# Chunk outputs added into y by accumulating transfers, and the gate row spread through DRAM, in a one-core SSD and gating-MLP layer

## The chip, the core and the metric

The kernel runs on one core of a Trainium2 chip. The metric is the time of one execution on the device in microseconds (us). The engines are PE (TensorE, matmuls into PSUM), DVE (VectorE), ACT (ScalarE), POOL (GpSimd) and SP (SyncE, which here only issues transfers). POOL and ACT issue transfers too.

## The reference, cut to what matters

One layer mixes 256 latent tokens (width 2048) with a prefix of 256 context tokens. An input projection feeds two groups of heads: a bidirectional Mamba-2 SSD (32 heads of 64, 8 groups of 4 heads) and a gating MLP. Both go through one output projection.

```python
zx = hx @ w_in                                   # f32; every product here is f32
xbc = silu(dwconv5(z[..., :XBC_W]))              # x heads, B, C of the SSD
# SSD in chunks of 128, per head, forward and backward:
y_diag = einsum('bcgqk,bcgrqk,bckgrp->bcqgrp', CB, Lmat, xdt)
y_off  = einsum('bcqgn,bcgrpn,bcqgr->bcqgrp', Cc, h_starts, exp(acs))
y = y_diag + y_off                               # both directions summed
y = y + d_skip * xh
y_a = rmsnorm(y * silu(z_ssd), g_ssd)
...
shift, scale, gate = split(silu(c) @ w_ada + b_ada, 3)
out = x + gate * rmsnorm(concat([y_a, y_b]) @ w_out, g_post)
```

`Lmat` is the causal decay between the tokens of a chunk. The kernel takes `gate * g_post` as one row `G` of 2048 numbers, repeated over the 128 partitions.

## The kernel before

**Matmuls.** An f32 product is made of three fp32r matmuls: the weights and the activations are each split into a high part (ACT casts, L543 or L87) and a low part (DVE subtracts, L549 or L88), and hi x hi, hi x lo and lo x hi are summed. The whole program is a long row of such matmuls, and everything else is set beside it. Weights come in blocks of 1 MB on SP's queue, four in flight; halves of a block are split ahead of PE, with four buffers.

**Stages.** First the modulation and the first seven projection tiles (to about 121 us). Then the 25 remaining tiles of x, B and C (`REST`), 512 columns each (256 for the C tiles), one after another into two PSUM banks (`acp`, bufs=2). Then 16 blocks of the latent-only projections (v, u and the two gate paths), then the output projection.

**The SSD beside the projection.** Group g owns the tiles 4g to 4g+3: two of x, one of B, one of C. For each tile `conv_tile` sets a first tap (ACT, L608), the other taps (DVE, L624) and a SiLU (ACT, L627). Tiles 12, 13 and 15 were projected in the first stage and wait in SBUF (`zq`, which lies in y's memory). Each is then turned so that tokens are on partitions. Groups 0 and (mostly) 7 do that on PE; groups 1 to 6 by DVE's 32x32 transpose, a store to DRAM (`turn`, SP) and four loads back (`turned`, SP). Then, per group: `ssd_cb` and `ssd_states` on PE, `ssd_mb` on POOL (M, L897), `ssd_hd` on POOL (hs, L885), `ssd_hl` on DVE (L891), `ssd_m` on DVE (L905, L907), `ssd_o` on PE, `ssd_yo` on DVE, `ssd_ya` on POOL (adds into y, L935), `ssd_yd` on PE (the diagonal part, into `psy`). The diagonal part comes out with heads on partitions, so it is turned as well: `ssd_yc`, `ssd_yt`, and `ssd_yf` adds it to y (DVE, L972).

The decay of group g+1 is prepared in between. `row_load` (POOL, L725) spreads 1 MB of cumulative sums into the one buffer `R`; `ssd_d` (ACT, L821) subtracts; `ssd_min` (DVE, L828) takes the minimum of two directions; then `row_load` of the next group may go; `ssd_e` (ACT, L834) is the exponential.

**Order.** PE, DVE, ACT and POOL run in the order in which this stage issues. It is made by a clock of the kernel's own: `later(t, f)` puts f into a list, due at the present clock plus t, and after every six matmuls `pump` advances the clock by 1.3 (0.65 in the 256-column tiles) and issues what is due, earliest due first. `plan_tile` sets all due times of a tile and `plan_d`, `plan_e` those of the decay. An engine waits at an instruction until its inputs are there, and all that is behind it on that engine waits too. SP's order and, after this stage, that of the other engines but for PE's sequence in the code are chosen by the framework.

**The gate.** `gate_tile` makes 16 columns of gate values on DVE. `gate_bcast` (L1076 on) transposes them on PE, splits them into two parts on ACT and DVE, and in four steps (`spread`) multiplies a matrix of ones with them on PE, so that every partition gets the row; the result is multiplied into `G`, which held `g_post`.

**y** is a tile of 128 x 4 x 2 x 512 (four pairs of groups, two chunks, 512). Transfers in `lat_t` turn it later, blocks of 128 at a time.

Of the kernel before, what the change touches and what calls it, by code (L numbers as in the profile page):

```python
# [36 lines left out]
C_BADA, C_GPRE, C_GSSD, C_GMLP, C_BS, C_CW, C_CB, NPC = 0, 48, 64, 80, 96, 112, 272, 304  # L37
# [10 lines left out]
def tile_hybrid_ssd_mlp(  # L48
# [47 lines left out]
    y = ypool.tile([P, 4, 2, 512], F32, tag="big16", name="y")  # L96
# [35 lines left out]
    gate = cpool.tile([P, 48], F32, name="gate")  # L132
# [21 lines left out]
    def yseg(j):  # L154
        return y[:, j % 4, j // 4]
# [589 lines left out]
    def turned(dst, D):  # L745
        for b in range(4):
            nc.sync.dma_start(dst[32 * b : 32 * b + 32].rearrange("p (u c) -> p u c", c=32),
                                D[16 * b : 16 * b + 16, :].rearrange("u (i c) -> i u c", c=32))
# [75 lines left out]
    def ssd_min(g, c):  # L824
        R = rows_[g]
        if c == 0:
            gs_.setdefault(g, {})["E"] = cv1.tile([P, 2, 4, P], F32, tag="E", name=f"E{g}")
        nc.vector.tensor_tensor(gs_[g]["E"][:, c], R[:, :, 0, c, :], R[:, :, 1, c, :], op=ALU.min)  # L828
        if c == 1:
            row_load(g + 1)  # L830
# [78 lines left out]
    def yg(g, c):  # L909
        return y[:, g // 2, c, (g % 2) * 256 : (g % 2 + 1) * 256]  # L910
# [40 lines left out]
    def ssd_yc(g):  # L951
        S = gs_[g]
        S["yc"] = cv1.tile([P, 2, 2, P], F32, tag="M", name=f"yc{g}")
        if by_pe(g, "y"):
            nc.scalar.copy(S["yc"], S["psy"])
        else:
            S["Dy"] = turn(S["yc"].rearrange("p c q k -> p (c q k)"), S["psy"].rearrange("p c q k -> p (c q k)"), f"y{g}")

    def ssd_yt(g):
        S = gs_[g]  # L960
        if not by_pe(g, "y"):
            S["pty"] = cv1.tile([P, 2, 2, P], F32, tag="yo0", name=f"yz{g}")
            turned(S["pty"].rearrange("p c q k -> p (c q k)"), S["Dy"])
            return
        S["pty"] = spt([P, 2, 2, P], f"pty{g}")
        for c in range(2):
            for q in range(2):
                nc.tensor.transpose(S["pty"][:, c, q, :], S["yc"][:, c, q, :], ident)
# [7 lines left out]
    def plan_tile(i, src, d0=0.0, ds=5.2, tx=7.0, tw=1.5, late=0.0, td=0.0):  # L976
# [3 lines left out]
        lx, lb, ly = (0.7 if by_pe(g, w) else LAND for w in (f"x{r}", "b", "y"))  # L980
# [41 lines left out]
    plan_tile(12, zq[0], 70, ds=7, tx=9)  # L1022
# [52 lines left out]
    def gate_bcast():  # L1075
        gs.close()  # L1076
        gp = ctx.enter_context(mkpool(name="gp", bufs=1, side="right"))
        G = gp.tile([P, D], F32, name="G")
# [3 lines left out]
        nc.vector.tensor_copy(gate[:, 32:48], gate[:, 0:16])


        gh = gp.tile([48, P], F32R, name="gh")
        gl = gp.tile([48, P], F32R, name="gl")
        g1 = gp.tile([48, P], F32R, name="g1")
        gd = gp.tile([48, 4, P], F32R, name="gd")
        gk = gp.tile([48, KT], F32, name="gk")
        nc.scalar.copy(g1, ones[0:48])  # L1090
        nc.vector.tensor_tensor(gk, ident[0:48, 0:16], ident[0:48, 32:48], op=ALU.add)

        def rows():
            ps = spt([48, P], "psgt")
            nc.tensor.matmul(ps, lhsT=gate, rhs=ident, start=True, stop=True)
            nc.scalar.copy(gh, ps)
            nc.vector.tensor_tensor(gl, ps, gh.bitcast(F32), op=ALU.subtract)
            nc.vector.tensor_copy(gh[32:48], gl[32:48].bitcast(F32))

        def expand(j):  # L1100
            nc.vector.tensor_tensor(gd, bc(gh.bitcast(F32), 1, 4), bc(gk[:, 4 * j : 4 * j + 4], 2, P), op=ALU.mult)

        def spread(j):
            p = spt([P, 512], f"pg{j}")
            nc.tensor.matmul(p, lhsT=g1, rhs=gd, start=True, stop=True)
            gb = G[:, j * 512 : (j + 1) * 512]
            nc.vector.tensor_tensor(gb, p, gb, op=ALU.mult)
            if j < 3:
                expand(j + 1)

        later(2, rows)
        later(4, lambda: expand(0))
        for j in range(4):
            later(7 + 3 * j, lambda j=j: spread(j))

    def lat_t(kind, j4):
        src = (L_["vt"] if kind == 2 else y)[:, j4]
        T = L_["lt2"].tile([P, 1024], F32, tag="gw", name=f"T{kind}{j4}").rearrange("p (u c) -> p u c", c=P)
        for tk in range(2):
            nc.vector.transpose(T[:, 4 * tk : 4 * tk + 4].rearrange("p u c -> p (u c)"), src[:, tk])  # L1120
        dst = src.rearrange("p t (j c) -> p (t j) c", c=P)
        for a in range(4):
            for b in range(4):
                nc.gpsimd.dma_start(dst[32 * b : 32 * b + 32, :, 32 * a : 32 * a + 32],  # L1124
                                    T[32 * a : 32 * a + 32, :, 32 * b : 32 * b + 32])
# [245 lines left out]
_INS = ["xch", "xtok", "ccols", "crow", "wada", "pcols", "dtp", "dskip", "gpost", "gv", "wst", "wxbc", "wlat", "wsp", "wout"]  # L1371
# [72 lines left out]
```

## Time and profile before

| | us |
|---|---|
| median of 3 runs (968.04 to 968.32) | 968.29 |
| the profiled execution | 968.23 |
| its span | 966.5 |
| DMA issues of `yz<-Dy` (SP), median to landing | 2.6 |
| `ssd_yf`'s adds (DVE), median | 0.68 |

The span is the profile's; what lies between it and the execution's time (1.7 us) is start and end. Lines of the timeline give the start, the duration, the engine, the line of the kernel, the operation, the tiles (out<-in), the shape and the count; in brackets stand the idle time of that engine before it and what ended that. A matmul's duration is longer than the step to the next one, since matmuls overlap: to price matmuls, read from start to start.

### The profile page before, as it was taken

The page shows a single profiled execution, that of the slowest core. Times are in us where ns is not written, and L with a number is a line of the kernel's source. Part 1 is how long each engine was busy: PE and PEld are TensorE (multiplying, and loading weights), DVE is VectorE, ACT ScalarE, POOL GpSimd, SP SyncE. Part 2 cuts the span into 40 slices and gives each one's busy share as a digit, 9 for nine tenths or more (in the row PEclk, how much of TensorE's full clock was granted, in tenths as well). Part 3 has the DMA queues.
Part 4 walks back from the last instruction along what each step waited for, and adds up shares of the span by engine and source line. Part 5 has one row for each costly group of instructions (what it writes and reads, how often), then busy time and mean ns, then how long its engine had stood idle before and what let it go on. Part 6 is the DMA issues. An engine that isn't in the chain of part 4 may idle for free.

```text
span 966.5 us, 13778 instructions
## 1 busy us (share of the span) xinstructions
PE 954.9 (99%) x5142; PEld 771.1 (80%) x5142; DVE 686.7 (71%) x1116; ACT 482.2 (50%) x732; POOL 192.5 (20%) x290
## 2 busy tenths in 40 slices
PE   9999999999999999999999999999999999999997
PEld 4688888777787878787888888887888888888885
DVE  6888798879887877866667687767666665445636
ACT  4344458554555544455445333455566564346512
POOL 0000002532533414323000000043335440000000
PEclk9999999999999999999999999999999999999999
DMA  9999965566659767647877767785666666556722
GB/s 367 416 416 415 371 228 166 145 187 156 136 151 229 170 179 163 164 143 248 317 295 281 285 259 273 285 302 197 198 226 214 215 214 216 198 181 255 261 87 87
DMA packets 141490, 224.57 MB, mean 232 GB/s; under 512 B 110816, under 2 KB 111072, under 8 KB 118768
## 3 DMA queue, kind: packets, MB, share of 16 engines
q1 hardware_dynamic: 134640, 206.03, 63.2%
q0 software_dynamic: 6208, 16.85, 5.6%
q8 instruction: 40, 0.66, 0.3%
q10 hardware_dynamic: 576, 0.82, 0.2%
q14 instruction: 26, 0.21, 0.1%
HBM read 210.76 MB, written 8.72 MB: 227 GB/s over the span
## 4 chain that ended last, share of the span: by engine, by line
PE 83%; DVE 7%; DMA 5%; issue 1%; SPq 1%; POOL 1%; ACT 1%; DVEq 0%; POOLq 0%; ACTq 0%
PE pa L1219 12%; PE pa L1220 12%; PE pa L1221 12%; PE psx L141 7%; PE psx L142 6%; PE psx L143 6%; PE pm L1260 3%; PE pm L1261 3%; PE pm L1262 3%; DMA ada<-in_wada_dram 3%; DVE xbc L624 3%; PE pq L1262 2%; PE pq L1260 2%; PE pq L1261 2%; PE psada L254 2%
## 5 line engine op out<-in xcount | busy, mean ns | idle before, releaser
L88 DVE TENSOR_TENSOR lo_w<-w,hi_w 128x1024 fp32r<-128x1024 f32 x173 | 210.5, 1222 | 138.1 <-ACT hi_w L87 137.9
L87 ACT CAST hi_w<-w 128x1024 fp32r<-128x1024 f32 x173 | 181.9, 1053 | 211.1 <-PE pa L1221 139.3
L1219 PE MATMUL pa<-hi_w,hhi 128*128 128x512 f32 x512 | 201.1, 393 | 0.0
L1221 PE MATMUL pa<-hi_w,hlo 128*128 128x512 f32 x512 | 199.3, 389 | 0.0
L1220 PE MATMUL pa<-lo_w,hhi 128*128 128x512 f32 x512 | 199.3, 389 | 0.0
L141 PE MATMUL psx<-hhi,hi_w 128*128 128x512 f32 (+1 forms) x400 | 151.5, 379 | 0.2 <-DVE xbc L624 0.2
L143 PE MATMUL psx<-hhi,lo_w 128*128 128x512 f32 (+1 forms) x400 | 145.7, 364 | 0.0
L142 PE MATMUL psx<-hlo,hi_w 128*128 128x512 f32 (+1 forms) x400 | 145.6, 364 | 0.0
L1219 PEld LDWEIGHTS pa<-hi_w,hhi 128*128 128x128 f32 x512 | 96.1, 188 | 21.2 <-issue 1.6
L1221 PEld LDWEIGHTS pa<-hi_w,hlo 128*128 128x128 f32 x512 | 96.1, 188 | 20.3
L1220 PEld LDWEIGHTS pa<-lo_w,hhi 128*128 128x128 f32 x512 | 96.1, 188 | 19.5 <-issue 0.2
L624 DVE SCALAR_TENSOR_TENSOR xbc<-psx,pc,xbc 128x248 f32<-128x248 f32 (+1 forms) x204 | 83.5, 473 | 26.0 <-ACT xbc L608 25.2
L549 DVE TENSOR_TENSOR lo_w<-w,hi_w 128x1024 fp32r<-128x1024 f32 x61 | 76.8, 1265 | 19.7 <-ACT hi_w L543 19.6
L141 PEld LDWEIGHTS psx<-hhi,hi_w 128*128 128x128 f32 x400 | 75.5, 189 | 14.8 <-issue 3.5
L142 PEld LDWEIGHTS psx<-hlo,hi_w 128*128 128x128 f32 x400 | 75.5, 189 | 12.9 <-issue 1.7
L143 PEld LDWEIGHTS psx<-hhi,lo_w 128*128 128x128 f32 x400 | 75.5, 189 | 12.3
L543 ACT CAST hi_w<-w 128x1024 fp32r<-128x1024 f32 x61 | 63.5, 1044 | 29.5 <-PE psx L142 16.6
L1260 PE MATMUL pm<-hi_w,hhi 128*128 128x512 f32 x128 | 49.8, 389 | 0.0
L1261 PE MATMUL pm<-lo_w,hhi 128*128 128x512 f32 x128 | 49.8, 389 | 0.0
L1262 PE MATMUL pm<-hi_w,hlo 128*128 128x512 f32 x128 | 49.8, 389 | 0.0
L1124 POOL DMA_DIRECT2D y<-T x64 | 36.8, 583 | 47.8 <-ACT sq L1195 33.1
L1124 POOL DMA_DIRECT2D vt<-T x64 | 36.8, 584 | 47.3 <-ACT sq L1195 34.8
(277 smaller groups left out, 1424.1 us busy)
## 6 DMA issues: line engine op xcount, KB each, us to landing
w<-in_wlat_dram SPq DMA_DIRECT2D x64, 1024.0 KB, 4.9
w<-in_wout_dram SPq DMA_DIRECT2D x32, 1024.0 KB, 4.8
w<-in_wxbc_dram SPq DMA_DIRECT2D x25, 1024.0 KB, 6.0
ada<-in_wada_dram SPq DMA_DIRECT2D x24, 1024.0 KB, 13.9
gate<-in_wada_dram SPq DMA_DIRECT2D x16, 1024.0 KB, 5.0
ada<-in_wada_dram SPq DMA_DIRECT2D x16, 512.0 KB, 12.4
R<-acs POOLq DMA_DIRECT2D x8, 1024.0 KB, 7.1
wst<-in_wst_dram SPq DMA_DIRECT2D x15, 480.0 KB, 13.0
```

The source lines that it names most:

```text
L87: nc.scalar.copy(hi, raw)
L88: nc.vector.tensor_tensor(lo, raw, hi.bitcast(F32), op=ALU.subtract)
L141: nc.tensor.matmul(ps, lhsT=whi, rhs=hhi[k][:, s], start=start, stop=False)
L142: nc.tensor.matmul(ps, lhsT=whi, rhs=hlo[k][:, s], start=False, stop=False)
L143: nc.tensor.matmul(ps, lhsT=wlo, rhs=hhi[k][:, s], start=False, stop=stop)
L624: nc.vector.scalar_tensor_tensor(ao, zi, cw[:, k : k + 1], ao, op0=ALU.mult, op1=ALU.add)
L1219: nc.tensor.matmul(pa[tk], lhsT=hhi[k][:, t], rhs=whi[:, w], start=k == 0, stop=False)
L1220: nc.tensor.matmul(pa[tk], lhsT=hhi[k][:, t], rhs=wlo[:, w], start=False, stop=False)
L1221: nc.tensor.matmul(pa[tk], lhsT=hlo[k][:, t], rhs=whi[:, w], start=False, stop=k == KT - 1)
L1260: nc.tensor.matmul(p, lhsT=yh[:, t], rhs=whi[:, w], start=j == 0, stop=False)
L1261: nc.tensor.matmul(p, lhsT=yh[:, t], rhs=wlo[:, w], start=False, stop=False)
L1262: nc.tensor.matmul(p, lhsT=yl[:, t], rhs=whi[:, w], start=False, stop=hf == 0 and j == 15)
```

## The change

1. `ssd_yc` always uses the DVE transpose and a store (`turn`), in groups 0 and 7 too; `ssd_yt` issues the four transfers of `turned` on POOL with an accumulating add, from DRAM into y itself. `ssd_yf` and its buffer go, and so do the transposes of `pty` on PE and the ACT copies of groups 0 and 7. The due time of `ssd_yt` is now the same in all groups.
2. y is laid out as 8 groups x 2 chunks x 256, so that a group is one run of 512. What reads y follows (`yg`, `lat_g`, `lat_split`, `lat_z`).
3. The gate: `g_post` comes as 16 columns in `pc`, is multiplied into the gate columns (DVE), stored to DRAM as a row (POOL, element by element) and loaded back repeated over the partitions (POOL). The PE, ACT and DVE work of `gate_bcast` goes.
4. The row load of group 5 is put 12 clock units after `ssd_min(4,1)` instead of right behind it.
5. Tile 12, which waits in SBUF, is planned at clock 63 instead of 70.

```diff
-    y = ypool.tile([P, 4, 2, 512], F32, tag="big16", name="y")
+    y = ypool.tile([P, 8, 2, 256], F32, tag="big16", name="y")
...
-    def turned(dst, D):
+    def turned(dst, D, q=nc.sync, **kw):
         for b in range(4):
-            nc.sync.dma_start(dst[32 * b : 32 * b + 32].rearrange("p (u c) -> p u c", c=32),
-                                D[16 * b : 16 * b + 16, :].rearrange("u (i c) -> i u c", c=32))
+            q.dma_start(dst[32 * b : 32 * b + 32].rearrange("p (u c) -> p u c", c=32),
+                        D[16 * b : 16 * b + 16, :].rearrange("u (i c) -> i u c", c=32), **kw)
...
         if c == 1:
-            row_load(g + 1)
+            later(12 if g == 4 else 0, lambda: row_load(g + 1))
...
     def ssd_yc(g):
         S = gs_[g]
-        S["yc"] = cv1.tile([P, 2, 2, P], F32, tag="M", name=f"yc{g}")
-        if by_pe(g, "y"):
-            nc.scalar.copy(S["yc"], S["psy"])
-        else:
-            S["Dy"] = turn(S["yc"].rearrange("p c q k -> p (c q k)"), S["psy"].rearrange("p c q k -> p (c q k)"), f"y{g}")
+        T = cv1.tile([P, 512], F32, tag="M", name=f"yc{g}")
+        S["Dy"] = turn(T, S["psy"].rearrange("p c q k -> p (c q k)"), f"y{g}")

     def ssd_yt(g):
...
-        S["pty"] = spt([P, 2, 2, P], f"pty{g}")
-        for c in range(2):
-            for q in range(2):
-                nc.tensor.transpose(S["pty"][:, c, q, :], S["yc"][:, c, q, :], ident)
-
-    def ssd_yf(g):
-        ya = y[:, g // 2, :, (g % 2) * 256 : (g % 2 + 1) * 256]
-        nc.vector.tensor_tensor(ya, ya, gs_[g]["pty"].rearrange("p c q k -> p c (q k)"), op=ALU.add)
+        turned(y[:, g].rearrange("p c x -> p (c x)"), gs_[g]["Dy"], nc.gpsimd, accum_op=ALU.add)
...
-                          (16.9 + td + (1.7 if ly < 1 else LAND + 3), ssd_yt), (18.6 + td + (0.7 if ly < 1 else 2 * LAND + 6), ssd_yf)]:
+                          (16.9 + td + LAND + 3, ssd_yt)]:
...
-    plan_tile(12, zq[0], 70, ds=7, tx=9)
+    plan_tile(12, zq[0], 63, ds=7, tx=9)
...
-        nc.gpsimd.dma_start(G, gpost.partition_broadcast(P))
-        nc.vector.tensor_tensor(gate[:, 0:16], gate[:, 0:16], pc[:, C_BADA + 32 : C_BADA + 48], op=ALU.add)
...
+        nc.vector.tensor_tensor(gate, gate, pc[:, C_BADA + 32 : C_BADA + 48], op=ALU.add)
+        nc.vector.tensor_tensor(gate, gate, pc[:, C_GPOST : C_GPOST + 16], op=ALU.mult)
+        row = drp.tile([16, P], F32, name="grow")
+        nc.gpsimd.dma_start(row.rearrange("j p -> p j"), gate)
+        nc.gpsimd.dma_start(G, row.rearrange("j p -> (j p)").unsqueeze(0).partition_broadcast(P))
```

More of the change, by code (lines that the diff above doesn't have):

```diff
@@ L36 @@
 WSSD = (0, 1, 2, 3, 4, 12, 5, 6, 13, 7, 8, 14, 9, 10, 15, 11)
-C_BADA, C_GPRE, C_GSSD, C_GMLP, C_BS, C_CW, C_CB, NPC = 0, 48, 64, 80, 96, 112, 272, 304
+C_BADA, C_GPRE, C_GSSD, C_GMLP, C_BS, C_CW, C_CB, C_GPOST, NPC = 0, 48, 64, 80, 96, 112, 272, 304, 320
 def _tile_order():
@@ L131, in tile_hybrid_ssd_mlp @@
     nc.vector.tensor_copy(bab[:, :, 1], pc[:, C_BADA : C_BADA + 16])
-    gate = cpool.tile([P, 48], F32, name="gate")
+    gate = cpool.tile([P, 16], F32, name="gate")
     nc.gpsimd.memset(gate, 0.0)
@@ L154, in yseg @@
     def yseg(j):
-        return y[:, j % 4, j // 4]
+        return y[:, 2 * (j % 4) + j // 4].rearrange("p c x -> p (c x)")
     zq = (yseg(2), yseg(3), yseg(7)[:, 0:256])
@@ L909, in yg @@
     def yg(g, c):
-        return y[:, g // 2, c, (g % 2) * 256 : (g % 2 + 1) * 256]
+        return y[:, g, c]
     def ssd_sk(g):
@@ L979, in plan_tile @@
         conv_tile(i, src, d0, ds)
-        lx, lb, ly = (0.7 if by_pe(g, w) else LAND for w in (f"x{r}", "b", "y"))
+        lx, lb = (0.7 if by_pe(g, w) else LAND for w in (f"x{r}", "b"))
         if lx == LAND:
@@ L1079, in gate_bcast @@
         L_["G"] = G
-        nc.gpsimd.dma_start(G, gpost.partition_broadcast(P))
-        nc.vector.tensor_tensor(gate[:, 0:16], gate[:, 0:16], pc[:, C_BADA + 32 : C_BADA + 48], op=ALU.add)
[L1082 to L1114, printed above, removed]
+        nc.vector.tensor_tensor(gate, gate, pc[:, C_BADA + 32 : C_BADA + 48], op=ALU.add)
@@ L1116, in lat_t, with lat_g @@
+        nc.vector.tensor_tensor(gate, gate, pc[:, C_GPOST : C_GPOST + 16], op=ALU.mult)
+        row = drp.tile([16, P], F32, name="grow")
+        nc.gpsimd.dma_start(row.rearrange("j p -> p j"), gate)
+        nc.gpsimd.dma_start(G, row.rearrange("j p -> (j p)").unsqueeze(0).partition_broadcast(P))
+    def lat_g(kind, j4):
+        if kind == 2:
+            return L_["vt"][:, j4].rearrange("p t x -> p (t x)")
+        return y[:, 2 * j4 : 2 * j4 + 2].rearrange("p g t x -> p (g t x)")
     def lat_t(kind, j4):
-        src = (L_["vt"] if kind == 2 else y)[:, j4]
+        src = lat_g(kind, j4)
@@ L1118, in lat_t @@
         T = L_["lt2"].tile([P, 1024], F32, tag="gw", name=f"T{kind}{j4}").rearrange("p (u c) -> p u c", c=P)
         for tk in range(2):
-            nc.vector.transpose(T[:, 4 * tk : 4 * tk + 4].rearrange("p u c -> p (u c)"), src[:, tk])
-        dst = src.rearrange("p t (j c) -> p (t j) c", c=P)
+            nc.vector.transpose(T[:, 4 * tk : 4 * tk + 4].rearrange("p u c -> p (u c)"), src[:, 512 * tk : 512 * tk + 512])
+        dst = src.rearrange("p (u c) -> p u c", c=P)
         for a in range(4):
@@ L1127, in lat_split @@
     def lat_split(kind, j):
-        src = (L_["vt"] if kind == 2 else y)[:, j // 4, :, (j % 4) * P : (j % 4 + 1) * P]
+        if kind == 2:
+            src = L_["vt"][:, j // 4, :, (j % 4) * P : (j % 4 + 1) * P]
+        else:
+            src = y[:, j // 2, :, (j % 2) * P : (j % 2 + 1) * P]
         if j % 4 == 0:
@@ L1184, in lat_z @@
     def lat_z(kind, j4, pa):
-        src = (L_["vt"] if kind == 2 else y)[:, j4]
         if kind == 3 and j4 == 0:
@@ L1191, in lat_z @@
             nc.scalar.activation(sz, pa[tk], AF.Silu)
-            tb = src[:, tk]
+            if kind == 2:
+                tb, sz = L_["vt"][:, j4, tk].unsqueeze(1), sz.unsqueeze(1)
+            else:
+                tb, sz = y[:, 2 * j4 : 2 * j4 + 2, tk], sz.rearrange("p (g x) -> p g x", g=2)
             nc.vector.tensor_tensor(tb, tb, sz, op=ALU.mult)
@@ L1368, in tile_hybrid_ssd_mlp @@
     man.close()
[L1371 removed]
+_INS = ["xch", "xtok", "ccols", "crow", "wada", "pcols", "dtp", "dskip", "gv", "wst", "wxbc", "wlat", "wsp", "wout"]
 _OUTS = [((256, 2048), "float32")]
```

9 lines of the change are left out of this document (1 added, 8 removed).

## The prediction

> **What bounds the kernel now.** I read first the busy times and the chain of work that ended last:
>
> ```profile
> PE 954.9 (99%) x5142; PEld 771.1 (80%) x5142; DVE 686.7 (71%) x1116; ACT 482.2 (50%) x732; POOL 192.5 (20%) x290
> PE 83%; DVE 7%; DMA 5%; issue 1%; SPq 1%; POOL 1%; ACT 1%; DVEq 0%; POOLq 0%; ACTq 0%
> ```
>
> TensorE (PE) works nearly always, so only two things count: matmuls taken off PE, and stretches in which PE waits. The change touches the SSD stage (135 to 450 us) and the gate spread (655 to 676 us). There the list of waits shows these of PE:
>
> ```profile
> PE psc L869 <- DMA bk<-Db: 2.8, 2, 1.4
> PE psx L141 <- DVE xbc L624: 0.2, 1, 0.2
> ```
>
> The second is the important one, small as it is. A projection tile accumulates in one of two PSUM banks (`acp`, bufs=2), so the tile after next starts only when VectorE (DVE) has done the convolution taps that read the bank. Here are PE's row, DVE's rows ahead of it, and the rows of GpSimd (POOL) and ScalarE (ACT) beside them, from the timeline:
>
> ```profile
> 219.53 0.47 PE L141 MATMUL psx<-hhi,hi_w 128*128 128x512 f32 x1 [0.22 <-DVE xbc L624]
> 190.16 0.68 DVE L828 TENSOR_TENSOR E<-R 128x512 f32<-128x512 f32 x1
> 198.80 1.00 DVE L891 TENSOR_TENSOR hs<-psl,hs 128x256 f32<-128x256 f32 x2 [1.46 <-POOL hs L885]
> 208.69 1.38 DVE L549 TENSOR_TENSOR lo_w<-w,hi_w 128x1024 fp32r<-128x1024 f32 x1
> 210.62 0.67 DVE L739 STREAM_TRANSPOSE yc<-psy 128x512 f32<-128x512 f32 x1
> 211.22 1.84 DVE L828 TENSOR_TENSOR E<-R 128x512 f32<-128x512 f32 x2
> 216.19 3.19 DVE L624 SCALAR_TENSOR_TENSOR xbc<-psx,pc,xbc 128x248 f32<-128x248 f32 x8 [3.13 <-ACT xbc L608]
> 220.44 6.08 DVE L624 SCALAR_TENSOR_TENSOR xbc<-y,pc,xbc 128x248 f32<-128x248 f32 x8
> 230.62 0.71 DVE L739 STREAM_TRANSPOSE tb<-xbc 128x512 f32<-128x512 f32 x1
> 197.15 1.03 POOL L897 TENSOR_TENSOR M<-cbb,dtt 128x512 f32<-128x512 f32 x1 [5.19 <-DVE cbb L860]
> 198.16 1.17 POOL L885 TENSOR_TENSOR hs<-hs,ed 128x256 f32<-128x256 f32 x2
> 208.26 4.25 POOL L935 TENSOR_TENSOR y<-y,yo 128x256 f32<-128x256 f32 x4 [5.51 <-DVE yo L927]
> 187.11 1.28 ACT L834 ACT_TABLE_LOAD   x1
> 190.87 1.06 ACT L834 ACTIVATE E<-E 128x1024 f32<-128x1024 f32 x1 [2.48 <-DVE E L828]
> 213.14 1.28 ACT L834 ACT_TABLE_LOAD   x1 [4.22 <-DVE E L828]
> ```
>
> The taps of tile 10 (216.19, ending 219.38) release PE at 219.53. From 198.80 to 213.06 no row of DVE has idle time before it. Its idle 3.13 us at 216.19 isn't spare either: ACT's exponential waits for the minimum at 211.22, and tile 10's first tap (L608) is queued behind that exponential. So DVE has **no slack** on this road: whatever is put on it from 188 us on starts the next tile later, microsecond for microsecond.
>
> **PE work removed.** Steps of PE, to be read start to start:
>
> ```profile
> 188.97 0.39 PE L143 MATMUL psx<-hhi,lo_w 128*128 128x512 f32 x1
> 189.20 0.60 PE L968 MATMUL pty<-ident,yc 128*128 128x128 f32 x4
> 190.79 0.40 PE L143 MATMUL psx<-hhi,lo_w 128*128 128x512 f32 x1
> 192.84 0.39 PE L143 MATMUL psx<-hhi,lo_w 128*128 128x512 f32 x1
> ...
> 656.54 0.39 PE L1221 MATMUL pa<-hi_w,hlo 128*128 128x512 f32 x1
> 658.47 0.40 PE L1221 MATMUL pa<-hi_w,hlo 128*128 128x512 f32 x1
> 662.56 0.39 PE L1221 MATMUL pa<-hi_w,hlo 128*128 128x512 f32 x1
> 665.93 0.39 PE L1221 MATMUL pa<-hi_w,hlo 128*128 128x512 f32 x1
> ```
>
> 190.79 to 192.84 holds 9 plain matmuls: 0.228 us each. 188.97 to 190.79 holds 6 of them and the four transposes of `pty`: 1.82 - 1.37 = 0.45 us, twice (groups 0 and 7). 656.54 to 658.47 holds 6 and the gate's transpose: 0.56. 662.56 to 665.93 holds 12 and one spread: 3.37 - 2.73 = 0.64, four times. In all 0.9 + 0.56 + 2.55 = **4.0 us** less on PE. The transpose at 189.2 saves nothing by itself, since PE waits for DVE at 219.53 anyway: 3.56 us count. The gate's ACT and DVE work lay beside PE work and is worth nothing.
>
> **What the SSD stage gains besides.** The DVE adds of `ssd_yf` go; none stands on the road above from 190.84 to 219.38. PE's other waits are these, with what led to the second:
>
> ```profile
> 240.72 0.67 PE L869 MATMUL psc<-xw,bk 128*128 128x512 f32 x1 [1.42 <-DMA bk<-Db]
> 303.66 0.67 PE L869 MATMUL psc<-xw,bk 128*128 128x512 f32 x1 [1.35 <-DMA bk<-Db]
> 291.86 0.59 POOL L725 DMA_DIRECT2D R<-acs  x1 [2.09 <-DVE E L828]
> 292.90 6.00 SPq L747 DMA_DIRECT2D bk<-Db  x4
> 337.64 1.91 SPq L747 DMA_DIRECT2D bk<-Db  x4
> R<-acs POOLq DMA_DIRECT2D x8, 1024.0 KB, 7.1
> 310.90 3.62 ACT L821 ACTIVATE R<-R,y 128x128 f32<-128x128 f32 x12
> ```
>
> At 291.86 the 1 MB row load of group 5 starts just ahead of group 4's `bk` issues, and these take 6.00 us against 1.91 in the next group. This is the load that is put 12 units later. By the order of issue POOL then meets it behind `ssd_sk(4)` and the four issues of group 3. Issued by 303 it lands, 7.1 us on, ahead of its reader at 310.90, and POOL has nothing else to do by then. I count the wait at 303.66 as gone (1.35); if the accumulations collide with `bk` in its place, it stays. The wait at 240.72 goes because PE comes later (below), if the `bk` of group 2 isn't later by as much (1.42). Together **-2.8**.
>
> The Trainium skill (DMA: Bandwidth & Descriptors, Issuing engines are not separate DMA queues) says that transfers issued from different engines share the same 16 DMA engines. By that rule the 24 transfers taken from SyncE's queue (SP) still crowd `bk`, and the wait at 303.66 could stay: 1.35 more than my sum.
>
> **What is put on the road.** The kernel's own clock gives the order of issue on POOL, DVE and ACT.
>
> (a) Group 0's copy of `psy` moves from ACT to a DVE transpose, ahead of `ssd_min(1,·)`: 0.60 by the step 210.62 to 211.22, partly won back as the split behind it meets less POOL work. I take 0.25, bounds 0 and 0.65.
>
> (b) The exponential of group 1 had its table load (1.28) done before its wait (187.11, 190.87); group 2's loads only after it (213.14). Before group 1's came an ACT copy that waited for PE, and it goes. Bounds 0 and 1.28; with nothing nearer I take 0.5.
>
> (c) `ssd_yt(0)` falls due at 55.4; `ssd_mb(1,0)` at 55.0 and `ssd_hd(1)` at 56.1. So four accumulating issues stand on POOL between 197.15 and 198.16, and DVE's row at 198.80 waits for the latter. The nearest price is that of POOL's other transfers of 128-byte pieces:
>
> ```profile
> L1124 POOL DMA_DIRECT2D y<-T x64 | 36.8, 583 | 47.8 <-ACT sq L1195 33.1
> 446.20 0.54 POOL L1156 DMA_DIRECT2D gw<-in_wsp_dram  x1
> Dy<-yc SPq DMA_DIRECT2D x6, 256.0 KB, 4.1
> ```
>
> 4 x 0.583 = 2.33. Their data, transposed ahead of the minimum at 190.16 and 4.1 us in landing, is there by 195. An accumulating issue isn't in this trace. By the code it has 512 pieces where `y<-T` has 256, so I bound one by the shortest issue of POOL (0.54) and twice 0.583: 2.2 to 4.7 for four. I take 2.33, from the row with the most similar pieces; R's 0.59 for 1 MB says that size matters little.
>
> (d) Tile 12's taps, due at 63.9 instead of 70.9, now stand right behind the split at 208.69 and ahead of `ssd_x(2,1)` (64.2), `ssd_yc(1)` (64.3) and `ssd_min(2,0)` (64.4). They read SBUF twice: 6.08 beside POOL work (220.44), 3.19 the like without (216.19). POOL's adds run 2.5 us past that split's end, so about half of the taps meet them: 4.6. The two minima then run without them, some 1.3 (twice 0.68, less their overlap) for 1.84. Net 4.0, bounds 2.6 and 6.0. They leave their old place behind tile 10's taps, where PE doesn't wait.
>
> So tile 10's taps end 0.25 + 0.5 + 2.33 + 4.0 = **7.1 us later**, and PE with them. Group 2's `tb` (230.62) comes only some 1.7 later (7.1, less the old 6.0 ahead of it, and 0.6 for tile 12's transpose, which now precedes it); hence no wait at 240.72.
>
> In the other groups the four issues fall into POOL's idle times: nothing, with the least cover in group 3.
>
> **At the stage's end** POOL loads `cb2` behind group 7's issues:
>
> ```profile
> 441.23 1.09 PE L947 MATMUL psy<-E,xk 128*64 128x128 f32 x16
> 445.09 0.59 POOL L1066 DMA_DIRECT2D cb<-in_crow_dram  x1
> 451.67 1.92 ACT L1067 ACTIVATE cb<-cb 128x2048 f32<-128x2048 f32 x1 [0.72 <-DMA cb<-in_crow_dram]
> ```
>
> Group 7's `psy` is ready at 442.3; one transpose, 4.1 us of transfer and 2.33 of issues put `cb2` some 5 us later, and ACT's activation stands ahead of weight casts for PE. Casts run about 8 us (three halves of 12 matmuls) ahead, and cast and split eat 2 to 3 of it. Bounds 0 and 2.5, taken 0.5, because the order of ACT is chosen anew there.
>
> **Sum** against the profiled execution (968.23, of which 966.5 are span; the median is 968.29): 7.1 - 3.56 - 2.8 + 0.5 = +1.2, so **969.5 us**. The gate row isn't in this trace. Its nearest row is the `Dy` store, which also has 2048 pieces and lands in 4.1 us; POOL waits that long between the store and the load of `G`, and behind it wait only `lat_t` issues, whose result is split 21 clock units after they are issued. `G` itself is first read after the output projection. I take 0, bounds 0 and 0.5 for the crowding of weight loads; without that cover it would be the two landings, some 11 us (4.1, and 6.6 by the steps of `cb2`). The y layout changes strides, not counts: 0.
>
> **Rivals.**
> 1. *The delay is not what holds PE* (0.28): the taps of tile 12 cost the road nothing, because DVE there waits for something that I don't see, or the order of issue is other than the clock gives. Then 3.1 - 3.56 - 2.8 + 0.5 = -2.8: 965.5. If nothing at all is put on the road: -4.0 - 0.2 - 2.8 = 961.3. For it: PE and the `bk` waits are in plain sight. Against: DVE's closed ranks from 198.80 on, and the 0.22 at 219.53.
> 2. *Accumulating issues hold POOL longer* (0.20), slower: between `M` and `hs` of group 1 they take 1.17 each for twice the pieces, +2.3, and as much again ahead of `cb2`, where 1 to 2 reach PE: 973.0. It turns the result to slower from about 0.76 us an issue. For it: twice the pieces, and a read of `y`. Against: R's 1 MB issues in 0.59. The Trainium skill (Perfetto Trace Analysis, DMA Instruction — SWDGE (GPSIMD)) says that such a row ends when the descriptors have been generated, which speaks for it; no run here shows an accumulating one.
>
> **Chances.** Forecast 0.52 (967.0 to 972.0; of it 0.02 faster, 0.32 same, 0.18 slower), rival 1 0.28 faster, rival 2 0.20 slower. Bound 0.2%, 1.94 us, about what a measurement here can tell: faster 0.30, same 0.32, slower 0.38. Range 963.0 to 973.5: it leaves out the end of rival 1 (0.08) and of rival 2 (0.08).
>
> **What would show it.** PE's wait on DVE's taps near 219 grows from 0.2 to some 7 us; DVE waits about 4 us for POOL's `hs` in group 1; four POOL rows near 199, 0.58 each; no `psc` wait. If PE has no wait near 219, the forecast is wrong and rival 1 holds; POOL rows over 0.76 mean rival 2.

## The result: 16 us slower, and the profile after

The changed kernel takes 984.65 us (median of five runs, 984.0 to 986.21), the kernel before 968.31: a ratio of 1.0169 (95% interval 1.0155 to 1.0183). A sixth run took 1937.12 us, far from all others, and is left out; with it the median is 985.25, the figure from which the expectations below start. The forecast was 969.5, in 963.0 to 973.5; the time lies above its upper end. The profiled execution took 986.21, its span is 984.5, and all numbers by place below are from it, against the span of 966.5 before.

First the view of what PE waited for, after the change; columns are the total in us, the count and the longest.

```profile
PE psx L140 <- DVE xbc L623: 6.0, 2, 4.8
PE pa L1183 <- ACT hi_w L86: 4.1, 1, 4.1
PE pso L920 <- DVE hs L890: 3.9, 1, 3.9
PE px L1326 <- ACT dg L1325: 1.5, 1, 1.5
PE pa L1184 <- DVE lo_w L87: 1.5, 2, 1.0
```

Both `psc` waits are gone, as forecast, and the wait on tile 10's taps (`psx <- xbc`) has grown from 0.2 to 4.8. Two waits stand there that the forecast doesn't have: `pso` for group 1's `hs` (3.9) and `pa`, in the later projection, for weight casts (4.1). Two smaller ones are new as well: 1.2 on the taps (the rest of the 6.0) and 1.5 for low parts of weights (`lo_w`). But what PE waits more than before, the 2.8 that are gone taken off, adds up to only some 12.5 of 18 us. The rest shows when one sets PE's milestones of both timelines beside each other:

| PE reaches | later than before by, us | added since the row above |
|---|---|---|
| group 0's `psc` | 0.35 | run to run |
| group 1's `psc` | -0.14 | the transposes of group 0's `pty` (0.45) gone |
| tile 14's first matmul | 10.2 | **the road to tile 10's taps** |
| group 2's `psc` | 10.6 | a stretch at half clock (below) +2.0, its old wait -1.6 |
| group 4's last product (`psy`) | 8.9 | its old `psc` wait -1.6 |
| group 5's `psc` | 10.3 | a new wait 1.2 at 339 and slow steps, +1.4 |
| the first `psg` (third stage) | 10.0 | the transposes of group 7's `pty` (0.4) gone |
| the third `psg` | 11.6 | two waits for splits, +1.6 |
| first half of the output projection | 15.6 | **the gate: PE work -3.1, waits and half clock +7** |
| its second half | 15.6 | nothing |
| the end | 18.0 | **a longer matmul step, +2.4** |

Now the road to tile 14, rows of the timeline after, in the order of the forecast's (b), (c), (d); in brackets the engine's idle time and what ended it:

```profile
191.44 1.28 ACT L833 ACT_TABLE_LOAD   x1 [5.32 <-DVE E L827]
199.94 4.43 POOL L746 DMA_DIRECT2D y<-Dy  x4
205.04 0.99 DVE L890 TENSOR_TENSOR hs<-psl,hs 128x256 f32<-128x256 f32 x2 [5.85 <-POOL hs L884]
216.23 4.67 DVE L623 SCALAR_TENSOR_TENSOR xbc<-y,pc,xbc 128x248 f32<-128x248 f32 x8
222.04 1.25 DVE L827 TENSOR_TENSOR E<-R 128x512 f32<-128x512 f32 x2
226.41 3.20 DVE L623 SCALAR_TENSOR_TENSOR xbc<-psx,pc,xbc 128x248 f32<-128x248 f32 x8 [3.13 <-ACT xbc L607]
229.75 0.77 PE L140 MATMUL psx<-hhi,hi_w 128*128 128x512 f32 x1 [4.78 <-DVE xbc L623]
```

All stand where the forecast put them. The table load comes after ACT's wait, whole: 1.28. The four issues take 4.43, **1.11 us each where 0.583 was taken**, and POOL's `hs` behind them comes as much later; DVE then waits 5.85. Tile 12's taps take 4.67 and the minima behind them 1.25, where two took 1.84. Tile 10's taps begin at 226.41 against 216.19, and PE's matmul behind them at 229.75 against 219.53. Of these 10.2 us PE spends a part earlier, at `pso`, so its wait for the taps themselves is 4.8 and not the 7 that the forecast named as its sign.

The next view is that of windows of 4 us on PE: the stretch and its length, busy time (instructions), granted clock (the share of full speed that TensorE is given; 0.50 is half clock), share and GB/s of the DMA engines.

```profile
202.00:206.00 4.00, 0.25 (x2) 1.00 1.41 116
206.00:210.00 4.00, 3.83 (x6) 0.58 0.19 12
...
226.00:230.00 4.00, 0.24 (x1) 0.64 0.94 244
230.00:234.00 4.00, 4.00 (x10) 0.51 1.61 210
...
676.00:680.00 4.00, 0.56 (x1) 0.71 0.31 50
680.00:684.00 4.00, 3.53 (x9) 0.50 0.73 186
```

Behind each of the three long waits PE is busy and yet does half: 10 matmuls in the window from 230, where 19 are usual, at a clock of 0.51. In windows of 1 us the clock is low from 206.6 to 210.0, from 227.1 to 233.9 and from 677.7 to 684.5: 3.4 us once and 6.8 us twice, and these two begin while PE still waits. What falls on PE's work is done at half speed (0.43 us from matmul to matmul where 0.23 is usual), so that each stretch costs about 2 us, a second price of a wait that no row of waits shows. It isn't always on the road: behind the wait at `pso`, tile 14 waits for DVE anyhow.

POOL and ACT at the gate, by the timeline after:

```profile
642.73 1.19 POOL L1067 DMA_DIRECT2D grow<-gate  x1 [81.50 <-DVE gate L1065]
657.15 0.55 POOL L1068 DMA_DIRECT2D G<-grow  x1 [13.24 <-DMA grow<-gate]
657.78 2.34 POOL L1083 DMA_DIRECT2D vt<-T  x4
667.24 0.58 POOL L1083 DMA_DIRECT2D vt<-T  x1 [5.40 <-DMA G<-grow]
676.75 1.70 ACT L1102 ACTIVATE hhi<-vt,gc 128x256 fp32r<-128x256 f32 x4 [10.58 <-DMA vt<-T]
678.36 3.87 ACT L86 CAST hi_w<-w 128x1024 fp32r<-128x1024 f32 x4
```

(The view of the third row ends at 660; three more of these issues follow it at once.) The store of the row and the load of G stand **ahead** of all transfers of T, though `gate_bcast` is issued a block later than the first of these. POOL waits 13.24 us for the store, whose data G's load reads. Seven issues of T go behind that load, and the eighth waits 5.40 for G to land; why it waits for that is not shown. The splits of T on ACT wait 10.58, the casts stand behind them in ACT's order, and PE waits for a cast. In the profile of before the same order could be read, at no price: PE has no wait there.

```profile
628.93 0.53 POOL L1080 DMA_DIRECT2D G<-in_gpost_dram  x1 [78.97 <-ACT sz L1191]
635.36 4.63 POOL L1124 DMA_DIRECT2D vt<-T  x8 [5.90 <-ACT hi_w L87]
```

Last the groups of matmuls of the output projection, both halves after, then the second half before (line, form, count, busy us, mean ns):

```profile
L1224 PE MATMUL pm<-hi_w,hhi 128*128 128x512 f32 x128 | 49.9, 390 | 0.0
L1224 PE MATMUL pq<-hi_w,yah 128*128 128x512 f32 x96 | 38.0, 396 | 0.0
```

```profile
L1260 PE MATMUL pq<-hi_w,yah 128*128 128x512 f32 x96 | 37.3, 389 | 0.0
```

Same shape, same clock (1.00), no wait, and 7 ns more. From start to start, 24 matmuls take 5.60 us in place of 5.44; 384 of these steps make 2.5 us.

### The profile page after: what moved, and what is told of

Read it like the earlier page. It is cut to its first block, busy times and chain, and to the rows that moved or that the text cites. A ratio compares the mean times of both kernels' runs of the same rounds, so it can differ in the third digit from the quotient of the medians.

```text
span 984.5 us, 13724 instructions
## 1 busy us (share of the span) xinstructions
PE 960.5 (98%) x5128; PEld 773.6 (79%) x5128; DVE 675.1 (69%) x1099; ACT 479.8 (49%) x728; POOL 228.2 (23%) x323
## 4 chain that ended last, share of the span: by engine, by line
PE 65%; DMA 19%; DVE 8%; issue 4%; ACT 1%; POOL 1%; SPq 0%; DVEq 0%; ACTq 0%; POOLq 0%
DMA gate<-in_wada_dram 10%; PE psx L140 8%; PE psx L141 8%; PE psx L142 8%; PE pa L1184 5%; PE pa L1185 5%; PE pa L1183 5%; PE pm L1225 3%; PE pm L1226 3%; PE pm L1224 3%; DMA ada<-in_wada_dram 3%; DVE lo_w L87 3%; PE pq L1226 2%; PE pq L1225 2%; PE pq L1224 2%
## 5 line engine op out<-in xcount | busy, mean ns | idle before, releaser
L1056 DVE SCALAR_TENSOR_TENSOR junk<-gate,cb 128x2048 bf16<-128x2048 f32 x16 | 36.7, 2293 | 45.8 <-DMA gate<-in_wada_dram 41.3
## 6 DMA issues: line engine op xcount, KB each, us to landing
wst<-in_wst_dram SPq DMA_DIRECT2D x15, 480.0 KB, 12.9
```

## The experiments

Each is timed against the kernel before on its own chip, whose median was 968.29 to 969.21 us; so kernels are compared by what they take over it, in the third column. "Changed" is the kernel after the change.

| kernel | us | over before, us | ratio to before, 95% interval |
|---|---|---|---|
| changed | 984.65 | +16.3 | 1.0155 to 1.0183 |
| a_yt0_late | 982.15 | +12.9 | 1.0115 to 1.0143 |
| a_t12_70 | 980.35 | +11.1 | 1.0098 to 1.0128 |
| a_gate_pe | 978.48 | +9.3 | 1.0077 to 1.0102 |
| a_r5_now | 987.61 | +18.4 | 1.0167 to 1.0219 |
| a_pad | 981.48 | +13.2 | 1.0118 to 1.0154 |
| a_noacc | 980.11 | +11.8 | 1.0102 to 1.0133 |
| a_gate_fast | 979.61 | +10.5 | 1.0083 to 1.0118 |
| a_three | 971.49 | +3.2 | 1.0021 to 1.0051 |
| a_three_dram | 976.95 | +8.7 | 1.0066 to 1.0094 |
| a_three_exp1 | 972.18 | +3.8 | 1.0029 to 1.0055 |
| a_three_anchor | 971.86 | +3.4 | 1.0023 to 1.0050 |
| a_y_only | 975.77 | +7.3 | 1.0063 to 1.0087 |
| b_t12_63 | 970.95 | +2.5 | 1.0012 to 1.0030 |
| b_shift64 | 970.19 | +1.7 | 1.0009 to 1.0026 |
| b_shift128 | 972.72 | +4.2 | 1.0026 to 1.0050 |
| b_gate | 968.34 | -0.1 | 0.9985 to 1.0007 |
| b_gate_r5 | 967.37 | -1.1 | 0.9978 to 0.9996 |
| b_best | 965.93 | -3.2 | 0.9952 to 0.9978 |

### One part undone at a time

```diff
a_yt0_late:
-                          (16.9 + td + LAND + 3, ssd_yt)]:
+                          (16.9 + td + LAND + 3 + (8.5 if g == 0 else 0), ssd_yt)]:
a_t12_70:
-    plan_tile(12, zq[0], 63, ds=7, tx=9)
+    plan_tile(12, zq[0], 70, ds=7, tx=9)
a_r5_now:
-            later(12 if g == 4 else 0, lambda: row_load(g + 1))
+            later(0 if g == 4 else 0, lambda: row_load(g + 1))
a_gate_pe: the gate's lines of the change undone, the inputs too
```

> The changed kernel with one edit: the four accumulating issues of group 0 fall due 8.5 clock units later, so that POOL meets them behind group 1's hs and M and behind the adds of its y. Theory (they took 4.4 us on the road to tile 14): DVE's wait for POOL's hs and PE's wait at pso in group 1, 3.9 us, go; tile 14 starts about 4.4 us sooner, and PE also loses less to the lower clock that follows a long wait; time 985.25 -> 979 to 981. Rival (the taps of tile 12 alone hold tile 14, and the issues only fill time that DVE would wait anyway): PE's wait moves from pso to tile 14's start, and the time stays within 1 us of 985.25.

> The changed kernel with tile 12 due at 70 again in place of 63. Theory (its taps, 4.67 less what the minima win back, are 4.0 us of the road): tile 14 starts about 4 us sooner, PE's wait there falls from 4.8 to about 1, and with less time at the lower clock behind it the whole is 4 to 5.5 us shorter: 979.5 to 981.5. Rival (what holds tile 14 is only the four issues): within 1 us of 985.25.

> The changed kernel with the gate row spread by TensorE again, as before. Theory (the 13 us store of the row and the load of G behind it hold back POOL's transfers of T, and these the splits and casts that PE waits for): PE's waits of 4.15 and 0.47 us near 680 and the slow stretch behind them (1.9) go, 3.1 us of PE work come back: 985.25 - 6.5 + 3.1 = 981.9, range 981 to 983. Rival (the transfers of T would be late all the same, because cb2 comes later and the gate's last tile with it): the waits stay and the work comes on top: 988.

> The changed kernel with the row of group 5 loaded at once, as before, in place of 12 units later. Theory (the later load bought PE's wait at psc of group 4, 1.6 us, and brought a wait of 1.2 us near 339, because POOL issues it behind accumulating issues and ACT waits 2.7 us for it): the first comes back and the second goes: 984.5 to 986.5. Rival (the wait near 339 has another cause): 986.5 to 987.5.

What the changed kernel takes over the one before falls by 3.4, 5.2 and 7.1 us, and rises by 2.1 in the last. The first two did on PE's road what was expected: with the issues later the wait at `pso` went whole, and PE reached group 2's `psc` 4.2 us sooner; with tile 12 later, 5.6 us sooner, half clock included. So both hold tile 14, one behind the other. The time of the first, 982.15, lies above its range all the same: PE still waits 5.2 us at tile 14, with half clock behind it. The gate gave twice the expected 3.4: in its profile the waits near 680 went, and so did the two waits for splits near the third `psg` (1.6) and the longer matmul step at the end (2.4). Why the waits for splits went isn't shown: a_y_only, with the same gate, has 1.0 us there. The longer step had to be looked into (below).

By its rows the later row load was a gain (the two intervals overlap): at once, the whole is above both expected ranges. My reason for the wait at 339 holds only in part. The rows of the changed kernel show how the load came to stand almost 10 us behind its minimum, which ends at 303.17:

```profile
310.26 4.37 POOL L746 DMA_DIRECT2D y<-Dy  x4 [4.90 <-DMA Dy<-yc]
312.89 2.34 POOL L724 DMA_DIRECT2D R<-acs  x1
322.64 3.63 ACT L820 ACTIVATE R<-R,y 128x128 f32<-128x128 f32 x12 [2.73 <-DMA R<-acs]
```

The load stands behind accumulating issues that wait for group 3's data. ACT then waits 2.73 for it. With the load at once ACT doesn't wait for it, but PE waits 1.65 at group 4's `psc`, and 0.7 of the wait near 339 stays: DVE waits 2.86 there for group 4's `hs`, which POOL makes behind the same issues.

### The longer step: 64 bytes of address

The gate tile is 128 bytes shorter in the change and `pc` 64 longer. So all tiles on the lower side of SBUF, weights, `hhi` and `hlo` among them, lie 64 bytes lower; `yah` and `yal` on the upper side stay. Only the second half of the output projection multiplies one side with the other.

```diff
a_pad (from the changed kernel):
-    cpool.tile([P, 64], F32, name="cpad")
+    cpool.tile([P, 80], F32, name="cpad")
b_shift64 (from before): [P, 64] -> [P, 48]
b_shift128 (from before): [P, 64] -> [P, 32]
```

> The changed kernel with an unused SBUF tile 64 bytes per partition longer, and nothing else, so that the tiles on the lower side of SBUF (weights and their split halves, hhi, hlo) lie at the addresses of before again: the gate tile is 128 bytes shorter in the change and the column tile 64 longer, so all of these moved by 64 bytes, while yah and yal on the upper side did not. Theory: in the second half of the output projection, the only stage with its stationary operand on one side and its moving operand on the other, a matmul step was 0.2333 us in place of 0.2267 because of that; it returns to 0.2267, and 384 of them make 2.5 us: 985.25 -> 982.7, with the stages before unchanged. Rival (the step is slow because of something else that the gate's new way does, such as its transfers): no change, 985.25.

> The kernel before with the unused tile 64 bytes per partition shorter and nothing else, so that weights, hhi and hlo lie 64 bytes lower against yah and yal, as in the changed kernel. Theory: the step of the second half of the output projection goes from 0.2267 to 0.2333 us, all else stays: 968.3 + 2.5 = 970.8. Rival (only the changed kernel's other parts make the address matter): 968.3.

> The same with the tile 128 bytes shorter. If only a shift by half of 128 bytes costs: 968.3, with the step at 0.2267. If any move away from the tuned place costs: 970.8 again.

The rows of one line's matmuls (min, median, max ns), of a_pad, b_shift64 and b_shift128 in this order:

```profile
L1224 PE MATMUL pq<-hi_w,yah x96: 389/389/390, 887.6 to 952.2; 128*128 128x512 f32 x96
```

```profile
L1260 PE MATMUL pq<-hi_w,yah x96: 393/396/398, 869.9 to 936.4; 128*128 128x512 f32 x96
```

```profile
L1260 PE MATMUL pq<-hi_w,yah x96: 390/393/404, 872.0 to 938.2; 128*128 128x512 f32 x96
```

The theory holds in both directions (a_pad takes 3.1 us less over before than the changed kernel, of which 2.4 by the milestones of this stage; b_shift64 goes from 968.48 to 970.19, +2.45 in this stage, -0.9 elsewhere). That half of 128 bytes is what matters falls: 128 bytes cost 2.1 there as well (and some 1.2 in other waits, by its profile, most of it at group 4's `psc`). The place was tuned, and any move that was tried off it costs. The first half of the output projection, with both operands on the lower side, takes 86.8 us from first to last matmul in before, after, a_pad and both shifted kernels: not the address of one operand, but that of one against the other makes the difference. What rule stands behind it stays open.

### What an accumulating issue costs

```diff
a_noacc:
-        turned(y[:, g].rearrange("p c x -> p (c x)"), gs_[g]["Dy"], nc.gpsimd, accum_op=ALU.add)
+        turned(y[:, g].rearrange("p c x -> p (c x)"), gs_[g]["Dy"], nc.gpsimd)
```

> The changed kernel with the same transfers from GpSimd's queue, but without the add: they overwrite y (its chunk output from the state and the skip term are lost from the output). Theory A (the add makes the issue dear): an issue falls from 1.09 us to about 0.58, DVE's wait for hs in group 1 shortens by 2 us, and the time by 2 to 3 us: 982.5 to 983.5. Theory B (the number of pieces, 512 against the 256 of the latent transfers, makes it dear): an issue stays at 1.09 us and the time within 1 us of 985.25.

The groups of POOL's issues (busy us; the mean of the first is of overlapping rows), changed, then a_noacc:

```profile
L746 POOL DMA_DIRECT2D y<-Dy x32 | 35.0, 1727 | 18.7 <-DMA Dy<-yc 18.7
```

```profile
L746 POOL DMA_DIRECT2D y<-Dy x32 | 20.9, 659 | 18.1 <-DMA Dy<-yc 14.9 <-issue 3.2
```

35.0 / 32 = 1.09 us with the add, 0.65 without it: theory A. Twice the pieces of `y<-T` cost 0.07 (0.583 to 0.65), the add 0.44. The time over before fell by 4.5, more than expected: group 1's wait at `pso` (2.1) brought no half clock, and the wait near 339 went too.

### One part alone, from before

```diff
b_t12_63 (from before):
-    plan_tile(12, zq[0], 70, ds=7, tx=9)
+    plan_tile(12, zq[0], 63, ds=7, tx=9)
a_y_only (from the changed kernel): a_t12_70, a_gate_pe and a_r5_now together
```

> The kernel before with tile 12 due at 63 in place of 70 and nothing else. Theory (its taps stand ahead of tile 10's on DVE in the closed rank, 4.0 us): tile 14 starts some 4 us later, PE's wait of 1.4 us at psc of group 2 goes, so 968.3 + 4.0 - 1.4 = 970.9, up to 972.5 where the wait at tile 14 brings a stretch at half clock. Rival (they cost only behind a late group 1, and fit in DVE's idle time without it): 968.3, within 0.7.

> The changed kernel with tile 12 at 70, the gate row by TensorE and group 5's row at once: what is left of the change are the y transfers. Theory: group 1's hs waits 4.4 us for the issues and the exponential's table load adds 1.3, so tile 14 starts 5 to 6 us later, the wait at psc of group 2 goes (1.4), 0.5 us of PE work go, and a stretch at half clock behind the wait at pso takes 1 to 2: 968.3 + 5.5 - 1.9 + 1.5 = 973.4, range 972 to 975. Rival (my 2.33 and 0.5 for these two terms, forecast of the prediction): 969.5.

Tile 12 alone gives 970.95 (expected 970.9): PE waits 3.8 us at tile 14, which starts 3.6 later, and the 1.4 at `psc` go. That the number fits so closely is in part luck, since two terms that the expectation left out cancel: a stretch at half clock behind the wait (+1.6), and the wait at group 4's `psc`, which goes too (-1.6). The y transfers alone give 975.77, past the expected range: group 1 is as late as in the changed kernel, half clock behind `pso` (0.50 in the window from 206, and on to 212.2) costs 3.0 us by the milestones, and the wait at group 2's `psc` doesn't go but grows, from 1.4 to 2.4.

### The gate row

```diff
a_gate_fast (from the changed kernel):
-        nc.vector.tensor_tensor(gate, gate, pc[:, C_GPOST : C_GPOST + 16], op=ALU.mult)
+        gr = gp.tile([P, 32], F32, name="gr")
+        gt = gp.tile([P, 32], F32, name="gt")
+        nc.vector.memset(gr, 0.0)
+        nc.vector.tensor_tensor(gr[:, 0:16], gate, pc[:, C_GPOST : C_GPOST + 16], op=ALU.mult)
+        nc.vector.transpose(gt, gr)
...
-        nc.gpsimd.dma_start(row.rearrange("j p -> p j"), gate)
+        for a in range(4):
+            nc.gpsimd.dma_start(row[:, 32 * a : 32 * a + 32], gt[32 * a : 32 * a + 16, :])
a_three_dram: a_yt0_late, a_t12_70 and a_pad; gate_bcast() called behind oproj(0, ...)
a_three_anchor: the same, and
+        nc.vector.tensor_copy(gr[:, 0:4], halves[max(halves)][0][:, 0:4].bitcast(F32))
b_gate: before, with a_three_anchor's gate and addresses; b_gate_r5: and a load of row 5 due 12 later
b_best: b_gate_r5 with a_gate_fast's store
```

> As the three edits together, but the gate row stays in DRAM: its store and load are put behind the first half of the output projection, and the unused tile is 64 bytes longer. Theory (the row's cost was only its place ahead of the transfers of T, and the addresses): 3.1 us of PE work go against the kernel with the gate by TensorE: 967.4, range 966.4 to 968.5. Rival (the row's transfers cost wherever they stand, by crowding the weight loads or by G coming late for the end): 969 or more.

> The kernel with issues later, tile 12 at 70 and the gate row in DRAM (976.95), but now the row is tied to a weight half that is split only in the second half of the output projection, so that its store and load come behind all transfers of T on GpSimd's queue; in 976.95 the framework had pulled them ahead of these though the code had them last. Theory (only the place on the queue cost): PE's waits of 2.9 and 2.5 us for the casts go, 3.1 us of PE work stay away: 971.49 - 3.1 = 968.4, range 967.4 to 969.4. Rival (a row in DRAM costs wherever it stands): over 970.

> The changed kernel with the gate column turned by one VectorE transpose of 32 columns before it is stored, so that the row goes to DRAM in four transfers of 16 pieces of 128 bytes, in place of one of 2048 pieces of 4 bytes; the store and the load of G stand at the same place on GpSimd's queue. Theory (the store's landing is what holds back the transfers of T): landing falls from 13 to 2 or 3 us, PE's waits near 680 and the half clock behind them go, 985.25 - 6.5 = 978.8, range 978 to 980. Rival (the load of G, 1 MB, is as bad): 982 to 985.

a_three_dram missed by 9.5 us, and its POOL row tells why: put in the code behind a whole stage, the store still ran at the old place. Its row, and that of a_three_anchor, where the store reads a tile that was made from a late weight half:

```profile
636.24 1.19 POOL L1067 DMA_DIRECT2D grow<-gate  x1 [81.35 <-DVE gate L1065]
```

```profile
871.04 1.17 POOL L1069 DMA_DIRECT2D grow<-gr  x1 [72.07 <-DVE gr L1067]
```

Outside the SSD stage, a clock in the code sets no order; only data do. Tied down, the row frees PE of its 3.1 us, but PE waits 0.7 in the second half of the output projection, and 971.86 is no better than with the gate by TensorE. So a place further down isn't free. The transfers by issue and landing (KB each, median us) show what is wrong with it, in the changed kernel and in a_gate_fast:

```profile
G<-grow POOLq DMA_DIRECT2D x1, 1024.0 KB, 9.8
grow<-gate POOLq DMA_DIRECT2D x1, 8.0 KB, 13.9
```

```profile
G<-grow POOLq DMA_DIRECT2D x1, 1024.0 KB, 6.7
grow<-gt POOLq DMA_DIRECT2D x4, 2.0 KB, 2.3
```

2048 pieces of 4 bytes take 13.9 us to land, 64 of 128 bytes 2.3. At the **same place** on the queue the waits near 680 go with that, PE's way from the third `psg` to the output projection is 3.2 us shorter than before, and the whole 979.61. The rest of a_gate_fast's distance is the address (2.4), the splits and the SSD stage.

### The three together, and what is left

```diff
a_three: a_yt0_late, a_t12_70 and a_gate_pe
a_three_exp1: the same, the unused tile cpad now named wrm_ and set to 0, and in ssd_e
+        if g == 1:
+            nc.scalar.activation(wrm_[:, 0:1], wrm_[:, 0:1], AF.Exp)
```

> The changed kernel with three edits together: group 0's issues 8.5 units later, tile 12 at 70, gate row by TensorE as before. Theory (the three are what the change cost, one after the other on one road: 3.1 + 4.9 + 6.8 by the single edits): 985.25 - 14.8 = 970.5, range 969.5 to 971.5, with psc waits coming back as PE comes sooner. Rival (the first two hide each other, and without both the road to tile 14 is free at once): under 969.5 if the sum of the two is more than the single edits show, 974 if they overlap.

> The kernel with the three edits (issues later, tile 12 at 70, gate by TensorE; 971.49) and one more: a one-column exponential on ACT ahead of group 1's exponential, so that the table is loaded while ACT waits for the minimum. Theory (the table load, 1.28 us behind that wait, is on the road to tile 14 and from there to group 2's bk): tile 14 and psc of group 2 come 1.0 to 1.3 us sooner, 970.2 to 970.5. Rival (psc of group 2 waits 3.0 us for bk whatever tile 14 does): PE's wait at psc grows by as much, and the time stays at 971.5.

Three parts undone take 13.1 of 16.3 us away, against 15.7 for the sum of the single ones; with intervals of some 1.4 us to either side on each, the difference can't be told from none. In a_three's profile the remaining 2.3 are: tile 14 some 1.9 later, group 2's `psc` wait at 3.0 (1.4 before), 1.1 near 330 for group 5's late row; against these 1.3 at group 4's `psc` and 0.9 of transposes.

The early table load did its part, with the offset at group 0 taken off: PE reached group 2's first product 1.2 us sooner and `psc` 1.0. But the wait there was 3.3 and not 3.0, and half clock followed it. Windows of a_three and a_three_exp1:

```profile
244.00:248.00 4.00, 4.00 (x15) 1.00 0.58 91
```

```profile
244.00:248.00 4.00, 4.00 (x9) 0.50 0.44 69
```

That cost 2.8 us and hid the gain, so the median shows nothing; term (b) is confirmed by place, not by time.

### A version faster than both

> The kernel before with the gate row in DRAM as its only change, tied in the same way behind the transfers of T, and with the addresses of before. Theory: 3.1 us of PE work go and nothing comes: 968.3 - 3.1 = 965.2, range 964.5 to 966. Rival (the work by TensorE was hidden, or the row costs as much as it saves): 967.5 or more.

> The same and the row of group 5 loaded 12 units later. Theory (no accumulating issues stand ahead of it here, so it lands in time, and PE's wait of 1.35 us at psc of group 4 goes): 965.2 - 1.35 = 963.9, range 963 to 964.6. Rival (the later row is late for ACT here too, and its wait comes back 25 us further on): 965 to 965.5.

> The kernel before with the gate row in DRAM, stored in that way and tied behind the transfers of T, addresses as before, row of group 5 later. Theory: the 0.8 us that PE waited in the second half of the output projection while 2048 small pieces went out are gone too: 967.4 - 0.9 = 966.5, range 965.2 to 967.2. Rival (that wait comes from G's load or from the split that the row is tied to): 967.4.

b_gate took the 3.1 us off PE and lost them again: 2.2 in the second half of the output projection, 0.9 of it as waits for splits, and 1.7 to half clock behind a `psc` wait of 2.0 us. In b_gate_r5 that wait stayed, against the theory. The rows of R's load, before and in b_gate_r5:

```profile
291.86 0.59 POOL L725 DMA_DIRECT2D R<-acs  x1 [2.09 <-DVE E L828]
```

```profile
294.61 0.59 POOL L724 DMA_DIRECT2D R<-acs  x1
```

Twelve clock units later in the order are 2.75 us later in time (0.9 of it because the minimum ends later): nothing on POOL waits in between, and the load still meets `bk`. It was the accumulating issues ahead of it that held it back in the changed kernel. With the store in 64 pieces the splits' waits go: **965.93 us, 0.22 to 0.48% faster than before**. It keeps of the change the gate row in DRAM, stored in larger pieces and tied to a later place, and the later row load, and leaves y's way and tile 12 as they were. What the later load brings in it isn't told: the two intervals of b_gate and b_gate_r5 overlap.

## Why the prediction was wrong, step by step

Between the forecast's +1.2 us and the profiled execution's +18.0 lie 16.8. By the milestones they are the gate row (7.1), the road to tile 14 (3.1 more than its 7.1), the longer matmul step (2.4), half clock behind tile 14's wait (2.0), the wait near 339 with the slow steps there (1.4) and the splits of the third stage (1.1 more than the 0.5 taken): 17.1 in all.

- **PE work off (-3.56)**: right. 0.49 and 0.37 by the milestones of groups 0 and 7, and 3.2 at the gate (a_gate_fast).
- **Both `psc` waits gone (-2.8)**: right as a sum in the changed kernel, and the half of it at group 4 was luck: that wait went for another reason than that given, not by 12 units, but by the wait of the issues ahead. This came back as PE's wait at 339 (1.2), where the forecast had the row land ahead of its reader. So "in the other groups the four issues fall into POOL's idle times: nothing" failed in group 3, whose issues waited 4.90 us for their data and held the row load.
- **The road to tile 14 (7.1)**: the order of the work and all four terms are where they were put; it measured 10.2, of which the rows of the four make 10.0. (a) 0.25: 0.2. (d) 4.0: 4.1 (taps of 4.67, less 0.59 at the minima), and 3.6 when made alone. **(c) was mis-sized: 2.33 taken, 4.43 measured.** I took the issue with the most similar pieces and left the add at nothing; the upper bound, 4.7, held. (b) was 1.28, its upper bound, where I took 0.5.
- **Rival 2** was the true one in this: it said 1.17 an issue and decided from 0.76. Its time was too low, because it left the rest as in the forecast.
- **The gate row (0, bounds 0 and 0.5)** is the step that failed, and the dearest. "Behind it wait only `lat_t` issues, whose result is split 21 clock units after they are issued" used the clock where the framework orders, and the profile of before had `G` ahead of `vt<-T` at 628.93. And the `Dy` store with as many pieces was no measure for pieces of 4 bytes: 13.9 us against 4.1. Price: 7.1 us with the half clock behind it.
- **`cb2` at the stage's end (0.5)**: `cb2` and with it the gate's tiles came later, but no wait stands there. The 1.6 us near the `psg` are waits for splits further on. They are not there in a_gate_pe, but a_y_only with the same gate has 1.0 of them: their cause stays open.
- **The layout (0)**: no row shows a price of y's strides. That the tile sizes move other tiles wasn't in the sum: 2.4.
- **No term for the clock**: a stretch at half clock behind a long wait, 2.0 of the sum at tile 14 and 1.9 at the gate.

By the rule of the Trainium skill that the prediction weighed (DMA: Bandwidth & Descriptors, Issuing engines are not separate DMA queues), that transfers share the same 16 DMA engines whichever engine issues them, `bk` can stay late although y's transfers leave SP's queue. The trace agrees where R, on POOL's queue, meets `bk`, on SP's: in a_r5_now, where y's transfers have left SP's queue and R goes at once, PE waits 1.65 us for `bk` at group 4's `psc`; in the changed kernel, where R comes later, there is none. The Trainium skill's other rule (Perfetto Trace Analysis, DMA Instruction — SWDGE (GPSIMD)), that such a row lasts until the descriptors are made, can't be weighed here: twice the pieces cost 0.07 more and the add 0.44, and no run shows what is made in that time.

## What to carry to other kernels

Price a DMA that its engine issues by its kind as well as by its pieces, bound it from above where the kind is new, and ask what stands behind it on that engine: this one cost 4.4 us in group 0, and in group 3 it held a row load that ACT then waited for. Ask for each stage who makes its order, the code or a scheduler, and read it in the timeline; a due time in the code moves a row along its queue, not in time. Look at the addresses when a tile changes its size, and count for a long wait of PE what it loses behind it.

## What the hardware showed that was not expected

- **Half clock behind a wait.** Waits of 3.8 us and more were followed by a stretch at a granted clock of about 0.5, 3.4 or 6.8 us long in the changed kernel, the wait's last part included. Shorter ones sometimes were: 1.9 us (b_gate_r5, 0.57 in the window from 304) and 3.3; but 2.3 (b_shift128) and 3.0 (a_three) not. The Trainium skill (TensorE: Matmul & The Clock Gate, Part 1: The HAM clock gate) says that activity is watched in windows of about 3.4 us that run free of the program, and that the clock is halved after one idle window. The length of the slow stretches (3.4 us or twice that) and the play of chance agree; that 1.9 us of waiting can do it does not, and there the measurement decides. It would fit the scatter of kernels with waits of 2 to 3 us, though only one execution of each was profiled: b_gate's runs go from 966.0 to 971.7.
- **An accumulating issue holds POOL 1.09 us**, the plain one 0.65.
- **64 bytes of SBUF address** between stationary and moving operand: 389 to 396 ns a matmul.
- **2048 pieces of 4 bytes** land in 13.9 us, 64 of 128 bytes in 2.3; the load that reads them waited, and POOL's later transfers stood behind it.
